# A two-layer trunk on one core: the weight sums begin after the rotated queries, and the bias rows are made in the plain stage

## The chip, the core and the metric

The kernel runs on one core of one Trainium2 chip. It uses the five engines of the core: PE (matrix products), DVE (vector), ACT (scalar functions and copies), POOL (a second vector engine) and SP, which here does nothing but issue transfers. ACT and POOL issue transfers too, each in its own queue and in the order of its other instructions. The metric is the time of one execution in device microseconds; less is better.

## The reference, cut to what matters

512 tokens of width 1024 go through two layers and a last norm. Layer 0 mixes tokens by two kinds of attention over all tokens, heads A (with rotated queries and keys) and heads B (through low-rank projections). Layer 1 uses a neighbourhood attention C whose scores get a bias from a small table, `od_rpb`, by the relative row and column of query and key. Each layer ends with an MLP with a squared ReLU.

```python
def sq_relu_mlp(h, w_up, w_down):
    u = jax.nn.relu(h @ w_up)
    return (u * u) @ w_down

h = x
for layer in range(2):
    hn = rmsnorm(h, norm_mix[layer])
    if layer % 2 == 0:
        h = h + hybrid_attention(hn, ...)            # heads A and B
    else:
        h = h + neighbourhood_attention(hn, od_w_qkv, od_rpb, od_w_out)
    h = h + sq_relu_mlp(rmsnorm(h, norm_ffn[layer]), ffn_w_up[layer], ffn_w_down[layer])
return rmsnorm(h, final_norm)
```

In the neighbourhood attention, `bias = rpb[:, kr - qr + ..., kc - qc + ...]` is added to the scaled scores of the keys in the window.

## The kernel before

Every fp32 product is made of three matmuls on PE: each operand is split into a rounded high part (`whi`, made by ACT) and the rest (`wlo`, made by DVE as operand minus high part).

The order of work is mostly that of the program; a scheduler puts each engine's instructions into a queue. The stages, with their times in the profile of before:

- **Heads A and B (from about 60 us on).** Per head and query tile: a pair of score matmuls (L1038), the exponential, transposes and value matmuls. Between them `fill` runs pieces of other products. `step(h, i)` is called once per head and tile. The queries of the second, third and fourth pair of heads are rotated on the way: SP swaps parts (L572), POOL multiplies (L576, L577), DVE adds, ACT rounds, DVE subtracts, and SP moves the halves into place by three transfers one after another (L649, L650, L651, in `sum_q`). The scores of those heads wait for the last of them; the tiles are named `a` and `sc`.
- **MLP, plain stage.** The first six row tiles of the up product and their part of the down product, as ordinary three-matmul products.
- **MLP, seven-product stage (about 328 to 482 us in layer 0, 900 to 1049 us in layer 1).** The rest of the up product goes by a scheme with seven block products instead of eight. It has 52 chunks in a layer. For each chunk (`seven_chunk`), SP loads a 128x2x256 piece of the weights (L300), POOL makes three sums of blocks (L302 to L304), ACT rounds (L308), DVE subtracts (L309), and PE runs 21 matmuls (L388 to L390).
- **MLP, sweeps (about 482 to 620 us in layer 0, from 1049 us on in layer 1).** The down product, in three kinds of sweep over pairs of row tiles kp (13 in layer 0, 11 in layer 1). It reads weights and sums of weight blocks from a tensor in device memory, `made`, splits them (L1310, L1311) and multiplies (L1413 to L1415).

**The sums ahead.** `SumsAhead` prepares `made` long before the sweeps. For each kp it issues two copies of 512 KB on ACT's queue (L809) and four accumulating transfers of 256 KB on POOL's (L803): two add a block of the weights (in the page `made<-in_ffn_w_down_dram`), and two add one block of `made` to another (`made<-made`), the second of which reads what the first wrote. It is a generator; `tick`, which every group of matmuls calls with its microseconds, advances it by one step when `every` microseconds have passed. These steps are the beats. For each kp the adds come one, two and three kp behind its copies, so that other steps lie between a transfer and the one that reads its result; where steps of one kind run out at the end of the list, the remaining adds follow one another directly. Both layers have such a list, `ahead0` with a beat of 4.7, set before the heads, and `ahead1` with 5.5.

**The bias rows.** `bias_rows` makes the rows of the bias for attention C: eight loads of the table by SP (L1264), two memsets and two copies on POOL (L1267 to L1271; L1270 copies a 128x128 part, L1271 a 128x248 part), and 48 stores to the device tensor `bx` on SP (L1276, L1280, L1282). In the kernel before, all of it is advanced by the sweeps of layer 0: one step for every fourth step of the sweeps of the second and third kind.

Working tiles come from a pool of 30 slots of 128x1024 elements (`Slot`) and from four raw buffers (`raw`); a chunk's load can go as soon as a slot is free and its place in SP's queue is reached.

Of the kernel before, what the change touches and what calls it, by code (L numbers as in the profile page):

```python
# [35 lines left out]
def encoder_kernel(ctx: ExitStack, tc: tile.TileContext, ins, out, dbg=None):  # L36
# [755 lines left out]
    class SumsAhead:  # L792
# [326 lines left out]
    def step(h, i):  # L1119
        n = count[0]  # L1120
        count[0] += 1
        if n == 35:
# [136 lines left out]
    def bias_rows():  # L1259
        held = tc.keep_in_program_order  # L1260
        R, Fi, Fe = Slot(F32), Slot(F32), Slot(F32)
        rpb = ins["od_rpb"][0]
        for qr in range(8):
            held(SP.dma_start(R.t[16 * qr : 16 * qr + 16, 0:248],  # L1264
                              rpb.rearrange("h a b -> h (a b)")[:, (7 - qr) * 31 : (7 - qr) * 31 + 248]))
            yield
        POOL.memset(Fi.t[:, 0:376], NEG)  # L1267
        POOL.memset(Fe.t[:, 256:512], NEG)
        rv = R.t[:, 0:248].rearrange("p (k d) -> p d k", d=31)
        POOL.tensor_copy(Fi.t[:, 0:376].rearrange("p (j k) -> p j k", k=8)[:, 15:31, :], rv[:, 7:23, :])  # L1270
        POOL.tensor_copy(Fe.t[:, 0:248].rearrange("p (j k) -> p j k", k=8), rv)  # L1271
        for _ in range(6):
            yield
        bxv = bx.rearrange("h t (c r) k -> t c r h k", r=8)
        for c in range(16):
            held(SP.dma_start(bxv[0, c].rearrange("r h k -> r h k"), Fi.t[:, (15 - c) * 8 : (15 - c) * 8 + 256]))  # L1276
# [3 lines left out]
            held(SP.dma_start(bxv[1, c][:, :, 128 * v : 128 * v + 128], Fe.t[:, off : off + 128]))  # L1280
            yield
            held(SP.dma_start(bxv[1, c][:, :, 128 - 128 * v : 256 - 128 * v], Fe.t[:, 256:384]))  # L1282
            yield
        for s_ in (R, Fi, Fe):
            s_.free()
        yield
# [192 lines left out]
    def mlp_swept(l, made, last=None):  # L1479
# [36 lines left out]
        for n, (kind, kp) in enumerate(sweeps[0].run(R)):  # L1516
# [3 lines left out]
            if kind and n % 4 == 0:  # L1520
# [266 lines left out]
    beat.update(every=5.5, work=ahead1.steps())  # L1787
# [169 lines left out]
```

## Time and profile before

| | |
|---|---|
| median of 3 executions | 1198.68 us (1196.86 to 1199.11) |
| the profiled execution | 1199.76 us |
| its span | 1197.9 us |
| PE busy | 1152.0 us, 96% |
| DVE busy | 905.0 us, 76% |
| ACT busy | 675.5 us, 56% |
| POOL busy | 527.5 us, 44% |

The span is the stretch from the first to the last instruction of one execution; 1.9 us of that execution lie outside it. A share over the span is a mean of stages: an engine with a small share can be the one that is waited for in one stage. A row of the timeline has the start in us, the duration, the engine, the line and the operation, and in brackets how long the engine was idle just before and what ended that. Rows at L803 on POOL, and rows of `SPq` and `ACTq`, are issues of transfers; their duration is that of the issue, not of the transfer.

### The profile page before, as it was taken

The numbers are of one execution on the slowest core, as the hardware profiler recorded it, in microseconds if no ns is written. First come the engines' busy times: TensorE is split into PE (matmuls) and PEld (weight loads), VectorE is DVE, ScalarE is ACT, GpSimd is POOL, SyncE is SP. The second block draws the span as 40 slices with busy tenths as digits, with TensorE's granted clock in tenths as the row PEclk, the third lists the DMA queues.
The fourth block names the chain that finished last, engine by engine and source line by source line (L and its number), as shares of the span: only waits on it lengthen the run. The fifth ranks groups of instructions, "written<-read, shape, count | busy, mean of one in ns | idle before, by whom it ended". The sixth has DMA issues, their size and how long they took to land.

```text
span 1197.9 us, 21331 instructions
## 1 busy us (share of the span) xinstructions
PE 1152.0 (96%) x7668; PEld 1040.3 (87%) x7668; DVE 905.0 (76%) x1627; ACT 675.5 (56%) x1157; POOL 527.5 (44%) x650
## 2 busy tenths in 40 slices
PE   9978999999999998998999999999999999999997
PEld 8657688888889998997998889988888999999995
DVE  5776899888967756994766566667889776699955
ACT  5456686665626655753653555554562665576625
POOL 3266454332699978032000332433169999800000
PEclk9998999999999998998999999999999999999999
DMA  7254464763876566826856867875667654685802
GB/s 250 62 146 114 131 159 102 180 141 109 242 188 157 152 131 131 292 84 205 256 155 169 228 184 185 196 170 154 195 158 212 161 138 121 154 254 177 265 10 70
DMA packets 131753, 197.33 MB, mean 165 GB/s; under 512 B 13011, under 2 KB 81536, under 8 KB 130880
## 3 DMA queue, kind: packets, MB, share of 16 engines
q1 hardware_dynamic: 113232, 138.18, 37.4%
q0 software_dynamic: 16128, 31.48, 16.5%
q10 hardware_dynamic: 2288, 26.32, 6.7%
q8 instruction: 60, 0.98, 0.4%
q14 instruction: 45, 0.37, 0.1%
HBM read 173.52 MB, written 56.62 MB: 192 GB/s over the span
## 4 chain that ended last, share of the span: by engine, by line
PE 64%; POOL 12%; DVE 10%; DMA 5%; issue 4%; ACT 3%; SPq 1%; ACTq 0%; POOLq 0%; DVEq 0%
PE mm L515 6%; PE mm L517 6%; PE mm L516 6%; POOL a L303 4%; POOL a L304 3%; PE s L1038 2%; POOL a L302 2%; PE t L1414 2%; PE t L1413 2%; PE t L1415 2%; PE o L1026 2%; PE t L1013 2%; POOL a L1270 1%; DMA raw<-in_ffn_w_down_dram 1%; PE s L516 1%
## 5 line engine op out<-in xcount | busy, mean ns | idle before, releaser
L309 DVE TENSOR_TENSOR wlo<-a,whi 128x896 fp32r<-128x896 f32 x98 | 121.5, 1241 | 72.9 <-ACT whi L308 66.8
L308 ACT ACTIVATE whi<-a 128x896 fp32r<-128x896 f32 x98 | 93.3, 952 | 129.7 <-POOL a L304 46.6
L515 PE MATMUL mm<-a,whi 128*128 128x512 f32 x395 | 160.0, 407 | 0.6 <-DVE sc L922 0.3
L517 PE MATMUL mm<-a,wlo 128*128 128x512 f32 x395 | 156.2, 396 | 0.4 <-DVE wlo L202 0.3
L516 PE MATMUL mm<-a,whi 128*128 128x512 f32 x395 | 156.2, 395 | 0.1
L202 DVE TENSOR_TENSOR wlo<-raw,whi 128x1024 fp32r<-128x1024 f32 (+4 forms) x87 | 100.7, 1162 | 32.1 <-ACT whi L212 32.0
L212 ACT ACTIVATE whi<-raw 128x1024 fp32r<-128x1024 f32 (+3 forms) x90 | 84.4, 942 | 66.1 <-PE s L516 13.6
L303 POOL TENSOR_TENSOR a<-a 128x256 f32<-128x256 f32 x98 | 95.2, 971 | 7.7
L517 PEld LDWEIGHTS mm<-a,wlo 128*128 128x128 f32 x395 | 74.4, 189 | 17.4 <-DVE wlo L202 1.3
L515 PEld LDWEIGHTS mm<-a,whi 128*128 128x128 f32 x395 | 74.4, 189 | 16.4 <-issue 1.1
L1046 POOL TENSOR_SCALAR p<-p,ti 128x512 f32<-128x512 f32 x64 | 47.8, 748 | 90.6 <-DVE ti L1045 72.1
L304 POOL TENSOR_TENSOR a<-a 128x128 f32<-128x128 f32 x98 | 84.2, 859 | 7.7
L302 POOL TENSOR_TENSOR a<-a 128x128 f32<-128x128 f32 x98 | 67.6, 690 | 44.6 <-DMA a<-in_ffn_w_up_dram 31.3
L516 PEld LDWEIGHTS mm<-a,whi 128*128 128x128 f32 x395 | 74.6, 189 | 13.5 <-DVE a L559 0.4
L388 PE MATMUL mm<-a,whi 128*128 128x256 f32 x280 | 79.7, 285 | 4.5 <-ACT whi L308 4.4
L1414 PE MATMUL t<-a,whi 128*128 128x256 f32 x288 | 81.0, 281 | 0.4 <-DVE a L1359 0.4
L390 PE MATMUL mm<-a,wlo 128*128 128x256 f32 x280 | 79.7, 284 | 1.6 <-DVE wlo L309 1.6
L1311 DVE TENSOR_TENSOR wlo<-a,whi 128x1024 fp32r<-128x1024 f32 x51 | 62.3, 1223 | 24.9 <-ACT whi L1310 24.8
L1413 PE MATMUL t<-a,whi 128*128 128x256 f32 x288 | 81.0, 281 | 0.0
L1415 PE MATMUL t<-a,wlo 128*128 128x256 f32 x288 | 80.7, 280 | 0.0
L389 PE MATMUL mm<-a,whi 128*128 128x256 f32 x280 | 79.4, 284 | 0.0
L1654 POOL TENSOR_SCALAR p<-p,ti 128x256 f32<-128x256 f32 x64 | 36.1, 575 | 96.7 <-DVE ti L1653 85.0
(395 smaller groups left out, 3927.8 us busy)
## 6 DMA issues: line engine op xcount, KB each, us to landing
a<-in_ffn_w_up_dram SPq DMA_DIRECT2D x98, 256.0 KB
made<-in_ffn_w_down_dram ACTq DMA_DIRECT2D x48, 512.0 KB
a<-made SPq DMA_DIRECT2D x74, 256.0 KB
made<-in_ffn_w_down_dram POOLq DMA_DIRECT2D x48, 256.0 KB, 5.3
made<-made POOLq DMA_DIRECT2D x48, 256.0 KB, 5.2
a<-in_ffn_w_down_dram SPq DMA_DIRECT2D x38, 256.0 KB
raw<-in_ffn_w_down_dram SPq DMA_DIRECT2D x34, 256.0 KB
raw<-in_ffn_w_down_dram SPq DMA_DIRECT2D x16, 512.0 KB
```

What stands on the lines that cost most here:

```text
L202: z = lambda: (eng or DVE).tensor_tensor(to, src, f32(high), op=ALU.subtract)
L302: POOL.tensor_tensor(r[:, 6], r[:, 0], r[:, 1], op=ALU.subtract)
L303: POOL.tensor_tensor(r[:, 4:6], r[:, 2:3].to_broadcast([P, 2, P]), r[:, 0:7:6], op=ALU.add)
L304: POOL.tensor_tensor(r[:, 7], r[:, 3], r[:, 5], op=ALU.subtract)
L308: ACT.activation(hi[:, 0:896], raw[:, 128:1024], AF.Copy)
L309: DVE.tensor_tensor(lo[:, 0:896], raw[:, 128:1024], f32(hi[:, 0:896]), op=ALU.subtract)
L515: PE.matmul(o, wh, xh, start=first, stop=False)
L516: PE.matmul(o, wh, xl, start=False, stop=False)
L517: PE.matmul(o, wl, xh, start=False, stop=last)
L1413: PE.matmul(o, wh, x[:, 0], start=first and m % 2 == 0, stop=False, skip_group_check=True)
L1414: PE.matmul(o, wh, x[:, 1], start=False, stop=False, skip_group_check=True)
L1415: PE.matmul(o, wl, x[:, 0], start=False, stop=last, skip_group_check=True)
```

## The change

There are two parts.

1. *The sums.* `ahead0` no longer begins before the heads: its beat is set in `step` at the count 20, which is the first query tile of head 5, right after the last rotated queries' transfers are in the program, and is 3.7 instead of 4.7. `ahead1`'s beat is 5.0 instead of 5.5. Behind the last kp's copies two empty beats are put ahead of each further kp's adds.
2. *The bias rows.* They take one slot, cut in three, instead of three slots. The POOL instructions are held in program order, one memset is 128 wide instead of 256, and the six empty steps between copies and stores are gone. Ten of the steps (the loads, the POOL work and the first store) are advanced in the plain stage's down product, and the other stores by every fifth step of the sweeps.

```diff
         def steps(self):
             for kp in range(self.n + 3):
+                if kp > self.n:
+                    yield
+                    yield
                 if kp < self.n:
                     for z in range(2):
                         tc.keep_in_program_order(ACT.dma_start(self.made[kp, z], self.w[kp, z]))
...
+        if n == 20:
+            beat.update(every=3.7, work=ahead0.steps())
         fill.run(1.5)
 
     ahead0, ahead1 = (SumsAhead(ins["ffn_w_down"][l], FIRST, RAW[l] // 2) for l in range(2))
-    beat.update(every=4.7, work=ahead0.steps())
...
     def bias_rows():
         held = tc.keep_in_program_order
-        R, Fi, Fe = Slot(F32), Slot(F32), Slot(F32)
+        slot = Slot(F32)
+        R, Fi, Fe = (slot.t[:, a:b] for a, b in ((0, 248), (248, 624), (624, 1008)))
         rpb = ins["od_rpb"][0]
         for qr in range(8):
-            held(SP.dma_start(R.t[16 * qr : 16 * qr + 16, 0:248],
+            held(SP.dma_start(R[16 * qr : 16 * qr + 16],
                               rpb.rearrange("h a b -> h (a b)")[:, (7 - qr) * 31 : (7 - qr) * 31 + 248]))
             yield
-        POOL.memset(Fi.t[:, 0:376], NEG)
-        POOL.memset(Fe.t[:, 256:512], NEG)
-        rv = R.t[:, 0:248].rearrange("p (k d) -> p d k", d=31)
-        POOL.tensor_copy(Fi.t[:, 0:376].rearrange("p (j k) -> p j k", k=8)[:, 15:31, :], rv[:, 7:23, :])
-        POOL.tensor_copy(Fe.t[:, 0:248].rearrange("p (j k) -> p j k", k=8), rv)
-        for _ in range(6):
-            yield
+        held(POOL.memset(Fi, NEG))
+        held(POOL.memset(Fe[:, 256:384], NEG))
+        rv = R.rearrange("p (k d) -> p d k", d=31)
+        held(POOL.tensor_copy(Fi.rearrange("p (j k) -> p j k", k=8)[:, 15:31, :], rv[:, 7:23, :]))
+        held(POOL.tensor_copy(Fe[:, 0:248].rearrange("p (j k) -> p j k", k=8), rv))
+        yield
...
         for c, gen in enumerate(gens):
             for i, _ in enumerate(gen):
                 later(c, i)
+                if i % 4 == 3 and c * 6 + i // 4 < 10:
+                    next(bias, None)
...
-            if kind and n % 4 == 0:
+            if kind and n % 5 == 0:
                 next(bias, None)
...
-    beat.update(every=5.5, work=ahead1.steps())
+    beat.update(every=5.0, work=ahead1.steps())
```

Lines shift: L1038 of before is L1041 of the change, L1267 to L1271 are L1272 to L1276, and the first store's L1276 is L1280. The rows below are read in the order in which the instructions stand in the queue of an engine. In them `a_3442` is the slot of the bias rows, `in_ffn_w_up_dram` the up product's weights, `made_621` and `made_622` are `made` of layer 0 and layer 1, and the other `a_` and `raw_` are chunks.

The first place is POOL's queue behind the sixth chunk of layer 0's seven-product stage. So it stands now; before, there was no instruction of the bias rows in this stage:

```order
L302 TENSOR_TENSOR a_3613<-a_3613 128x128
L303 TENSOR_TENSOR a_3613<-a_3613 128x256
L304 TENSOR_TENSOR a_3613<-a_3613 128x128
L1272 MEMSET a_3442 128x376
L1273 MEMSET a_3442 128x128
L1275 COPY a_3442<-a_3442 128x128
L1276 COPY a_3442<-a_3442 128x248
L803 DMA made_621<-in_ffn_w_down_dram 128x512
L302 TENSOR_TENSOR a_3690<-a_3690 128x128
L303 TENSOR_TENSOR a_3690<-a_3690 128x256
```

The two memsets and two copies have moved here from the sweeps, between two chunks' sums. In SP's queue the first store of `bx` that reads the result of these copies is followed by loads of chunks:

```order
L1280 DMA bx<-a_3442 8x16x256
L300 DMA raw_5040<-in_ffn_w_up_dram 128x2x256
L300 DMA a_3695<-in_ffn_w_up_dram 128x2x256
L300 DMA a_3726<-in_ffn_w_up_dram 128x2x256
L300 DMA raw_5169<-in_ffn_w_up_dram 128x2x256
L300 DMA a_3861<-in_ffn_w_up_dram 128x2x256
L300 DMA a_3825<-in_ffn_w_up_dram 128x2x256
```

Before, no store of `bx` stood among the loads of this stage.

The second place is POOL's queue near the end of that stage. Before:

```order
L803 DMA made_621<-in_ffn_w_down_dram 128x512
L302 TENSOR_TENSOR a_4786<-a_4786 128x128
L303 TENSOR_TENSOR a_4786<-a_4786 128x256
L304 TENSOR_TENSOR a_4786<-a_4786 128x128
L302 TENSOR_TENSOR a_4816<-a_4816 128x128
L303 TENSOR_TENSOR a_4816<-a_4816 128x256
L304 TENSOR_TENSOR a_4816<-a_4816 128x128
L803 DMA made_621<-made_621 128x512 x2
L302 TENSOR_TENSOR a_4884<-a_4884 128x128
L303 TENSOR_TENSOR a_4884<-a_4884 128x256
L304 TENSOR_TENSOR a_4884<-a_4884 128x128
L302 TENSOR_TENSOR a_4889<-a_4889 128x128
```

Now, at the place where the adds stand side by side:

```order
L803 DMA made_621<-made_621 128x512
L302 TENSOR_TENSOR a_4699<-a_4699 128x128
L303 TENSOR_TENSOR a_4699<-a_4699 128x256
L304 TENSOR_TENSOR a_4699<-a_4699 128x128
L803 DMA made_621<-made_621 128x512
L803 DMA made_621<-in_ffn_w_down_dram 128x512
L803 DMA made_621<-made_621 128x512
L302 TENSOR_TENSOR a_4768<-a_4768 128x128
L303 TENSOR_TENSOR a_4768<-a_4768 128x256
```

Before, two adds of `made` to `made` stood directly one behind the other, the second reading what the first writes; now one add stands after a single chunk's sums, followed further down by three adds in a row, of which the last reads what the one ahead of it writes.

The third place is POOL's queue in layer 1's seven-product stage, 13 chunks from its end. Before:

```order
L302 TENSOR_TENSOR a_11519<-a_11519 128x128
L303 TENSOR_TENSOR a_11519<-a_11519 128x256
L304 TENSOR_TENSOR a_11519<-a_11519 128x128
L803 DMA made_622<-made_622 128x512
L302 TENSOR_TENSOR a_11587<-a_11587 128x128
L303 TENSOR_TENSOR a_11587<-a_11587 128x256
L304 TENSOR_TENSOR a_11587<-a_11587 128x128
L302 TENSOR_TENSOR a_11592<-a_11592 128x128
```

Now:

```order
L302 TENSOR_TENSOR a_11389<-a_11389 128x128
L303 TENSOR_TENSOR a_11389<-a_11389 128x256
L304 TENSOR_TENSOR a_11389<-a_11389 128x128
L803 DMA made_622<-made_622 128x512 x2
L302 TENSOR_TENSOR a_11457<-a_11457 128x128
L303 TENSOR_TENSOR a_11457<-a_11457 128x256
L304 TENSOR_TENSOR a_11457<-a_11457 128x128
L302 TENSOR_TENSOR a_11462<-a_11462 128x128
```

The adds had a chunk or two of POOL's sums between them; now two of them stand side by side, and the second reads what the first writes. Fewer adds are left for the end of the stage.

More of the change, by code (lines that the diff above doesn't have):

```diff
@@ L1260, in bias_rows @@
         held = tc.keep_in_program_order
[L1261 removed]
+        slot = Slot(F32)
+        R, Fi, Fe = (slot.t[:, a:b] for a, b in ((0, 248), (248, 624), (624, 1008)))
         rpb = ins["od_rpb"][0]
         for qr in range(8):
[L1264 removed]
+            held(SP.dma_start(R[16 * qr : 16 * qr + 16],
                               rpb.rearrange("h a b -> h (a b)")[:, (7 - qr) * 31 : (7 - qr) * 31 + 248]))
             yield
[L1267 to L1273 removed]
+        held(POOL.memset(Fi, NEG))
[4 more added lines that the diff above has]
+        yield
         bxv = bx.rearrange("h t (c r) k -> t c r h k", r=8)
         for c in range(16):
[L1276 removed]
+            held(SP.dma_start(bxv[0, c].rearrange("r h k -> r h k"), Fi[:, (15 - c) * 8 : (15 - c) * 8 + 256]))
             yield
             v, off = (1, (7 - c) * 8) if c < 8 else (0, (23 - c) * 8)
[L1280 removed]
+            held(SP.dma_start(bxv[1, c][:, :, 128 * v : 128 * v + 128], Fe[:, off : off + 128]))
             yield
[L1282 removed]
+            held(SP.dma_start(bxv[1, c][:, :, 128 - 128 * v : 256 - 128 * v], Fe[:, 256:384]))
             yield
[L1284 to L1286 removed]
+        slot.free()
     def sweep_chunk(w, k0, kind, made):
```

## Prediction

> **What bounds the kernel now.** I read four views: the page's first part for the bound, the table of stretches for where the bound has holes, the list of PE's waits for what opens them, and the timeline around each hole. The first says that TensorE is the bound.
>
> ```profile
> span 1197.9 us, 21331 instructions
> PE 1152.0 (96%) x7668; PEld 1040.3 (87%) x7668; DVE 905.0 (76%) x1627; ACT 675.5 (56%) x1157; POOL 527.5 (44%) x650
> ```
>
> PE misses 1197.9 - 1152.0 = 45.9 us, and the change leaves its work alone: before and after it issues the same matmuls, in another order only among the heads of attention A. So the change can win at most part of 45.9 us, plus what half clock stretches, and can lose without limit. The stretches (columns: length, then busy time with instruction count of PE, PEld, DVE, ACT, POOL, then granted clock, DMA share, GB/s) show the holes:
>
> ```profile
> 60.00:90.00 30.00, 21.30 (x101) 15.35 (x99) 22.90 (x53) 16.14 (x33) 18.09 (x17) 1.00 0.55 146
> 90.00:120.00 30.00, 24.73 (x130) 21.17 (x131) 19.52 (x46) 18.20 (x41) 19.37 (x23) 0.85 0.46 115
> 390.00:420.00 30.00, 30.00 (x256) 30.00 (x255) 23.25 (x29) 18.70 (x23) 28.43 (x35) 1.00 0.61 159
> 420.00:450.00 30.00, 27.43 (x228) 26.81 (x226) 15.90 (x18) 15.05 (x17) 23.96 (x32) 1.00 0.58 124
> 450.00:480.00 30.00, 27.12 (x204) 26.82 (x205) 20.49 (x25) 17.36 (x21) 25.10 (x33) 0.89 0.64 136
> 540.00:570.00 30.00, 24.10 (x184) 23.40 (x183) 14.88 (x22) 12.01 (x18) 5.41 (x2) 0.89 0.67 214
> 990.00:1020.00 30.00, 30.00 (x258) 30.00 (x256) 19.43 (x24) 16.95 (x19) 28.27 (x37) 1.00 0.53 132
> 1020.00:1050.00 30.00, 28.09 (x231) 27.27 (x230) 20.51 (x24) 17.89 (x21) 23.03 (x30) 1.00 0.70 158
> 1110.00:1140.00 30.00, 30.00 (x256) 30.00 (x255) 26.68 (x40) 19.07 (x30) 0.00 (x0) 1.00 0.79 261
> ```
>
> Holes: heads A (60-120), the end of layer 0's seven-product stage (420-480), layer 0's sweeps (540-570), and a small one in layer 1's seven-product stage (1020-1050). POOL reads 28.43 and 28.27 of 30 in the two seven-product stages: it has no room there, whatever its 44% over the span says. Three waits open the large holes:
>
> ```profile
> PE s L1038 <- DMA a<-sc: 6.5, 2, 4.3
> PE mm L1413 <- ACT whi L1310: 4.7, 1, 4.7
> PE mm L388 <- ACT whi L308: 4.4, 1, 4.4
> ```
>
> Each of them also halves the granted clock for some time after (same columns):
>
> ```profile
> 90.00:97.00 7.00, 4.87 (x19) 4.40 (x20) 3.06 (x7) 1.67 (x4) 1.68 (x3) 0.52 0.32 78
> 117.00:121.00 4.00, 4.00 (x17) 3.27 (x16) 3.34 (x8) 2.52 (x6) 3.75 (x5) 0.58 1.02 258
> 452.00:459.00 7.00, 6.12 (x27) 5.83 (x28) 4.33 (x5) 2.61 (x4) 6.61 (x9) 0.51 0.42 81
> 551.00:558.00 7.00, 4.31 (x18) 4.02 (x19) 1.58 (x2) 2.07 (x3) 0.00 (x0) 0.51 0.92 314
> ```
>
> At clock 0.51, PE's 6.12 us hold about 6.12 x 0.49 = 3.0 us of work lost; the others 4.87 x 0.48 = 2.3, 4.00 x 0.42 = 1.7 and 4.31 x 0.49 = 2.1. A hole thus costs its idle time and some 2 to 3 us behind it.
>
> **Heads A: the sums leave.** Layer 0's sums started with the heads; now none is issued before head 5's first score. What PE waits for there is the rotation of the next queries, a relay of small transfers on SP's queue (L649 to L651), and L651 moves what the last copies need:
>
> ```profile
> 83.16 0.50 SPq L649 DMA_DIRECT2D a<-a  x1
> 87.67 0.46 SPq L651 DMA_DIRECT2D a<-sc  x1
> 92.13 1.65 PE L1038 MATMUL s<-a,a 128*128 128x512 f32 x3 [4.28 <-DMA a<-sc]
> 109.23 0.50 SPq L649 DMA_DIRECT2D a<-a  x1
> 113.11 0.46 SPq L651 DMA_DIRECT2D a<-sc  x1
> 116.70 0.73 PE L1038 MATMUL s<-a,a 128*128 128x512 f32 x2 [2.22 <-DMA a<-sc]
> ```
>
> The first relay takes 92.13 - 83.16 = 8.97 us, the second 116.70 - 109.23 = 7.47. Part of the difference is traffic: the first runs beside copies and sums, which now are gone. POOL, which makes the products that the rotation sums (L577), is not held by an add either, as it was here:
>
> ```profile
> 69.93 0.90 POOL L803 DMA_DIRECT2D made<-in_ffn_w_down_dram  x1 [0.73 <-DMA made<-in_ffn_w_down_dram]
> 70.55 1.58 POOL L577 TENSOR_TENSOR sc<-sc,a 128x512 f32<-128x512 f32 x1
> ```
>  The fill moves too: between the last scores of unrotated queries and the first that needs rotated ones, PE now has 11 matmuls of fill, 18 transposes and 16 value matmuls where it had 6, 12 and 9. The two waits, 6.5 us in sum, and the dips behind them, 2.3 and 1.7, are what can go: 10.5. Bounds: -10.5, and nothing, since the relay itself remains and 7.47 us of it is there with few sums beside it. I take **-6**, a little over half: the first wait loses 8.97 - 7.47 = 1.5 by the relay and more by the fill, and with it its dip; the second is left half of its 2.2 and 1.7.
>
> [...]
>
> **Layer 0's seven-product stage: POOL gets more.** A chunk here costs POOL three sums (L302 to L304), then ACT rounds, DVE subtracts, and PE multiplies. POOL's rows around the hole, with PE's:
>
> ```profile
> 443.32 0.81 POOL L803 DMA_DIRECT2D made<-made  x1
> 448.84 0.81 POOL L803 DMA_DIRECT2D made<-made  x1 [4.71 <-DMA made<-made]
> ...
> 453.89 0.81 POOL L803 DMA_DIRECT2D made<-made  x1
> 454.45 0.72 POOL L302 TENSOR_TENSOR a<-a 128x128 f32<-128x128 f32 x1
> ```
>
> ```profile
> 452.49 0.58 PE L388 MATMUL mm<-a,whi 128*128 128x256 f32 x1 [4.41 <-ACT whi L308]
> ```
>
> An add followed by the add that reads its result stands in POOL's order with nothing between; POOL waits 4.71 us for the first one's landing, and PE then waits 4.41. An add that does not wait costs POOL 454.45 - 453.89 = 0.56 us of its order. The change:
> - *The bias rows' memsets and copies* now stand behind the sixth chunk. Their durations are on these rows:
>
> ```profile
> 527.97 16.84 POOL L1270 COPY a<-a 128x128 f32<-128x128 f32 x1 [9.69 <-DMA a<-in_od_rpb_dram]
> 544.76 0.65 POOL L1271 COPY a<-a 128x248 f32<-128x248 f32 x1
> 528.00:544.80 16.80, 16.80 (x145) 16.80 (x144) 16.54 (x35) 10.55 (x21) 16.80 (x2) 1.00 0.05 17
> 340.00:350.00 10.00, 10.00 (x55) 8.54 (x54) 5.16 (x6) 1.91 (x2) 9.37 (x15) 1.00 0.93 240
> ```
>
>   The first copy took 16.84 us while DVE was busy 16.54 of 16.80; the second, with nearly twice the elements, 0.65 once DVE had stopped. Where they go now, DVE is busy 5.16 of 10. Bounds: 2 x 0.65 with DVE away, 16.84 + 0.65 with DVE full. 5.16 is a half-empty DVE, so I take the low end and double it, 2.7 us with the two memsets (an estimate, not rowed for the memsets).
> - *Adds*: 24 instead of 21 stand between the third and the last chunk: 3 x 0.56 = +1.7.
> - *Pairs*: the adjacent pair that waited 4.71 is gone, and another takes its place three chunks earlier (an add and the one that reads it, adjacent); one pair with only one chunk between is new. That chunk takes POOL some 2.6 us of a landing of about 4.71 + 0.81 = 5.5, so +2.5. These waits may come out between 0 and 4.71.
> - *SP's queue*: the first store of the rows waits for POOL's copy with seven weight loads behind it; with raw buffers loaded ahead I cost it at nothing. If the copy is as slow as 16.84, all of that cover is gone and it comes on top.
>
> Together POOL's end of the stage moves by 2.7 + 1.7 + 2.5 = 6.9. PE ran full until 420 (30.00 of 30), so POOL's lead of the early chunks hides little; I take **+6.5**, between +1 (POOL early enough, pairs landed) and +15 (slow copy).
>
> [...]
>
> **Layer 0's sweeps: the copy leaves.** The rows of that hole:
>
> ```profile
> 544.84 0.72 SPq L1276 DMA_DIRECT2D bx<-a  x1
> 547.02 1.82 SPq L1304 DMA_DIRECT2D a<-made  x4
> 553.23 0.58 PE L1413 MATMUL mm<-a,whi 128*128 128x256 f32 x1 [4.69 <-ACT whi L1310]
> ```
>
> The slow copy ended at 544.81, the store that needs it went at 544.84, and only then SP reached the sweep's loads at 547.02. PE misses 30 - 24.10 = 5.9 us in 540-570, about 1.1 behind it, and 2.1 at half clock: 9.1. With the copies done a stage earlier, SP's stores wait on nothing of POOL's. Layer 1's sweeps have no bias rows, and there PE is at 30.00 of 30 (1110-1140, DMA share 0.79). The stores' own issue time (0.72 us above) is spread more thinly (every fifth step). Bounds: -9.1 and -6 (a few loads late). I take **-8.6**.
>
> **Layer 1's seven-product stage.** With a beat of 5.0 for 5.5 the adds come earlier. Before, none waited in the stage, as this shows:
>
> ```profile
> 1042.64 1.65 POOL L803 DMA_DIRECT2D made<-made  x2
> 1049.44 0.81 POOL L803 DMA_DIRECT2D made<-made  x1 [5.15 <-DMA made<-made]
> ```
>
> The 5.15 us wait stands behind the last chunk and holds nobody. Now a pair stands adjacent inside the stage, 13 chunks from its end: up to 5.15 us of POOL, less the one add fewer (22 for 23, -0.56): +4.6. PE idles 1.9 there before (1020-1050), so POOL's lead is small but not zero until about 1020; I take **+4**, between -1 (landed in time, fewer adds late) and +7 (with a clock dip as above).
>
> **The plain stages and the tail** I cost at nothing. The sums' traffic of layer 0 is compressed by 4.7 / 3.7 = 1.27 in time after the heads, beside full PE (cover: loads issued ahead); uncovered, one late load would be a wait as in the sweeps, up to 4.7. The empty beats act after the last kp has been copied.
>
> **Sum**, against the profiled execution (1199.76 us, 1.1 above the median of 1198.68): -6 + 6.5 - 8.6 + 4 = -4.1, so 1195.7, rounded to 1195.5.
>
> **Rivals.**
> - *POOL's lead covers.* Both new waits land in time and the copies are short, so layer 0's stage costs +1 and layer 1's 0: -6 - 8.6 + 2 = -12.6, 1187. For it: before, PE did not idle until after 420, so a lead exists. Against: 28.43 of 30 busy.
> - *Slower: the copy meets DVE.* In its new place the first copy (L1275 of the change) runs long as L1270 did. Price: 16.84 for some 1.3, 15.5 more on POOL; if a lead of two chunks (5.5) covers a part, +10, so -4.1 + 10 = +6, 1206. It decides from a copy of some 5.4 us on, where the sum of -4.1 is eaten. For it: the old row. Against: DVE 5.16 of 10.
> - *The relay is the wait, not the traffic.* The heads' waits stay as they are (the change doesn't do there what it moves the sums for): term 0, sum +1.9, 1202. For it: 7.47 us in the relay with few sums beside it. Against: more fill ahead of the first such score.
>
> **How the numbers follow.** Forecast 0.45 (own range 1190 to 1201), POOL's lead 0.22, relay 0.18, copy 0.15. About what this kernel's measurement can tell is 0.2%, 2.4 us. Faster: 0.7 of the forecast and all of the lead, 0.54. Within: a quarter of the forecast and half of the relay, 0.20. Slower: the rest, 0.26. The range reaches to the two outer rivals, 1186 to 1206.
>
> **What would show it.** Right: no L803 on POOL before the sixth head, and the row at L1038 that waits for a<-sc under 3 us with no half clock behind it; the first copy (L1275) under 2 us, in the seven-product stage; no store of bx in the sweeps that waits for POOL and 540-570 above 29; in both seven-product stages a wait of PE at L388 of 2 to 6 us behind an L803 of 3 to 5. Wrong: a copy of over 5 us, PE full in the seven-product stages, or the relay's waits unchanged.

## The result, and the profile after

The changed kernel takes 1193.05 us (median of 5, 1192.06 to 1194.29) against 1198.68 us before (5 runs, 1196.86 to 1200.67): a ratio of 0.9953 with a 95% interval of 0.9939 to 0.9968. The forecast was 1195.5 us, with a range of 1186 to 1206 and faster as the likelier sign.

The page's first part of the kernel after, and then its two largest waits of PE (us in total, times, longest):

```profile
span 1192.5 us, 21335 instructions
PE 1152.1 (97%) x7668; PEld 1039.8 (87%) x7668; DVE 900.7 (76%) x1627; ACT 674.1 (57%) x1157; POOL 509.1 (43%) x650
```

```profile
PE s L388 <- ACT whi L308: 6.6, 1, 6.6
PE mm L390 <- DVE wlo L309: 4.5, 9, 1.1
```

PE has as much to do as before (1152.1 us), so all of the 5.4 us are holes closed or opened. The two waits for the rotated queries (6.5 us) and the wait in the sweeps (4.7 us) are gone from the list; the one at L388 in the seven-product stage is still there and has grown from 4.4 to 6.6. The stretches (columns as before: length, busy time of PE, PEld, DVE, ACT, POOL, granted clock, DMA share, GB/s):

```profile
60.00:90.00 30.00, 25.99 (x125) 19.45 (x123) 25.80 (x61) 19.49 (x39) 18.65 (x18) 0.94 0.21 55
90.00:120.00 30.00, 28.56 (x164) 22.53 (x164) 25.06 (x64) 25.38 (x58) 23.73 (x27) 1.00 0.34 89
150.00:180.00 30.00, 26.13 (x149) 22.34 (x148) 24.37 (x59) 21.90 (x49) 14.62 (x19) 0.94 0.71 176
420.00:450.00 30.00, 20.91 (x150) 19.39 (x149) 12.31 (x15) 11.28 (x14) 21.59 (x30) 0.90 0.63 114
540.00:570.00 30.00, 30.00 (x256) 30.00 (x255) 25.48 (x40) 18.62 (x30) 0.00 (x0) 1.00 0.73 232
990.00:1020.00 30.00, 28.58 (x237) 27.95 (x236) 18.69 (x21) 16.39 (x20) 25.32 (x33) 1.00 0.51 116
```

Heads A and the sweeps are fuller, 420-450 emptier. Fixed stretches mislead once the kernels have shifted against each other, so I also cut each profiled execution at the same pieces of work: the first matmul of each seven-product stage (L388), the first and the last matmul of each down product's sweeps. The lengths of the pieces, in us (layer 0's seven-product stage so begins at 347.5 us in the kernel before, later than in the list of stages, since the other engines work on its chunks ahead of PE):

| piece | before | after | difference | forecast |
|---|---|---|---|---|
| start to layer 0's seven-product stage | 347.5 | 340.4 | -7.0 | -6 |
| layer 0's seven-product stage | 138.2 | 148.0 | +9.8 | +6.5 |
| layer 0's sweeps | 139.2 | 128.9 | -10.3 | -8.6 |
| to layer 1's seven-product stage | 296.2 | 298.1 | +1.9 | 0 |
| layer 1's seven-product stage | 131.7 | 132.2 | +0.5 | +4 |
| layer 1's sweeps and the tail | 145.1 | 144.9 | -0.2 | 0 |
| sum, of the span | | | -5.4 | -4.1 |

The signs of the four terms came out as forecast; one of them, +0.5, is too small to tell from the spread between profiles (below). The stretch of layer 0's seven-product stage, cut so, before and after:

```profile
347.47:485.69 138.22, 132.76 (x1094) 131.85 (x1092) 97.12 (x115) 81.16 (x100) 117.62 (x148) 0.98 0.63 152
```

```profile
340.44:488.42 147.98, 135.41 (x1094) 131.93 (x1092) 99.88 (x119) 81.24 (x101) 122.84 (x154) 0.98 0.67 163
```

PE stands idle there for 5.5 us before and 12.6 us after, and its 1094 matmuls take 2.65 us longer. Half clock does not explain these 2.65 us: the granted clock is 0.98 in both rows, and the stretch at half clock is not longer than the one before the change (452 to 459 us, 6.12 us of matmuls):

```profile
444.00:450.83 6.83, 4.46 (x19) 4.17 (x20) 3.44 (x4) 3.07 (x4) 6.44 (x10) 0.50 0.35 76
```

What lengthens the other matmuls is not shown. The timeline of the kernel after shows the hole, POOL first and then PE:

```profile
427.47 0.81 POOL L803 DMA_DIRECT2D made<-made  x1
432.03 0.81 POOL L803 DMA_DIRECT2D made<-made  x1 [1.16 <-DMA made<-made]
434.62 0.80 POOL L803 DMA_DIRECT2D made<-made  x1
435.16 1.09 POOL L803 DMA_DIRECT2D made<-in_ffn_w_down_dram  x1
442.32 0.81 POOL L803 DMA_DIRECT2D made<-made  x1 [6.06 <-DMA made<-in_ffn_w_down_dram]
```

```profile
445.98 0.58 PE L388 MATMUL s<-a,whi 128*128 128x256 f32 x1 [6.63 <-ACT whi L308]
```

The last of three adds in a row waits 6.06 us for the one just ahead of it, and PE 6.63 for the chunk behind. Two adds with one chunk between wait 1.16.

### The profile page after: what moved, and what is told of

Its sections match the earlier page's. It is cut to its first block, busy times and chain, and to the rows that moved or that the text cites. A ratio compares the mean times of both kernels' runs of the same rounds, so it can differ in the third digit from the quotient of the medians.

```text
span 1192.5 us, 21335 instructions
## 1 busy us (share of the span) xinstructions
PE 1152.1 (97%) x7668; PEld 1039.8 (87%) x7668; DVE 900.7 (76%) x1627; ACT 674.1 (57%) x1157; POOL 509.1 (43%) x650
## 4 chain that ended last, share of the span: by engine, by line
PE 69%; POOL 12%; DVE 7%; DMA 4%; issue 4%; ACT 3%; ACTq 0%; POOLq 0%; SPq 0%; DVEq 0%
PE mm L515 6%; PE mm L517 6%; PE mm L516 6%; POOL a L303 5%; POOL a L304 3%; POOL a L302 3%; PE t L1416 3%; PE t L1415 3%; PE t L1417 3%; PE s L1041 3%; PE o L1029 2%; PE t L1016 2%; PE mm L1417 2%; DMA a<-in_ffn_w_up_dram 2%; PE mm L1415 2%
## 5 line engine op out<-in xcount | busy, mean ns | idle before, releaser
L308 ACT ACTIVATE whi<-a 128x896 fp32r<-128x896 f32 x95 | 89.6, 949 | 121.0 <-POOL a L304 59.2
L303 POOL TENSOR_TENSOR a<-a 128x256 f32<-128x256 f32 x95 | 89.3, 943 | 7.3
L302 POOL TENSOR_TENSOR a<-a 128x128 f32<-128x128 f32 x95 | 72.3, 764 | 40.8 <-DMA a<-in_ffn_w_up_dram 40.3
L1566 POOL DMA_DIRECT2D a<-a x16 | 8.7, 547 | 179.3 <-PE mm L516 164.4
L1313 DVE TENSOR_TENSOR wlo<-a,whi 128x1024 fp32r<-128x1024 f32 x56 | 68.3, 1222 | 21.3 <-ACT whi L1312 20.9
L388 PE MATMUL mm<-a,whi 128*128 128x256 f32 x280 | 78.7, 281 | 0.2 <-ACT whi L308 0.2
```

The lines of the kernel that those rows point to most:

```text
L302: POOL.tensor_tensor(r[:, 6], r[:, 0], r[:, 1], op=ALU.subtract)
L303: POOL.tensor_tensor(r[:, 4:6], r[:, 2:3].to_broadcast([P, 2, P]), r[:, 0:7:6], op=ALU.add)
L308: ACT.activation(hi[:, 0:896], raw[:, 128:1024], AF.Copy)
```

## The experiments

The theory to be tested: four places, each with its own cause, whose effects add; and in the seven-product stages the cost is the wait of an add for the one issued just before it. The main rivals: POOL's whole work paces those stages, so that the wait only shows where the lack falls; and what one place gains, the next gives back.

Each experiment's time stands beside runs of the kernel before on the same chip (medians 1197.8 to 1198.3), and the ratio is to these.

### Each part alone

Only the sums' part (the bias rows as before):

```diff
-    beat.update(every=4.7, work=ahead0.steps())
+        if n == 20:
+            beat.update(every=3.7, work=ahead0.steps())
... (and the empty beats, and 5.0 for 5.5)
```

> Only the change's part on the sums (start at head 5's first score, beats 3.7 and 5.0, empty beats); the bias rows as before, made and stored in the sweeps. By the theory (four places, each with its own cause, that add): heads A gain 7 us as in the change, the sweeps keep their whole hole (first wait of about 4.7 us at L1413 behind a POOL copy of about 17 us), and layer 0's seven-product stage has an adjacent dependent pair of adds at chunk 39, so it stays near its 138 us or rises by up to 5: 1192 to 1197, near 1194. Rival (the heads' gain is only idle time that the next stages give back, so the sum is set by the stages' POOL): within 2 us of the kernel before.

Measured: 1194.92 us (10 runs), ratio 0.9975 (0.9955 to 0.9995). The sweeps keep their hole, as the rows of its timeline show, POOL's and then PE's:

```profile
528.98 17.87 POOL L1274 COPY a<-a 128x128 f32<-128x128 f32 x1 [8.65 <-DMA a<-in_od_rpb_dram]
```

```profile
554.57 0.39 PE L1417 MATMUL mm<-a,whi 128*128 128x256 f32 x1 [4.00 <-ACT whi L1314]
```

Its sweeps take 137.8 us, and its seven-product stage 140.7, with a wait of POOL of 5.42 us at an adjacent pair and one of PE of 5.95 us behind it. Its profiled execution, the slowest of the ten, gains almost nothing up to the stage (346.9 us), mostly because of one wait of 4.54 us for a transfer in heads B that the other kernels with the sums begun at head 5 show at 0 to 1.8 us. So the gain of the heads cannot be read from this profile.

Only the bias rows' part (the sums as before):

```diff
+        slot = Slot(F32)
+        R, Fi, Fe = (slot.t[:, a:b] for a, b in ((0, 248), (248, 624), (624, 1008)))
... (and the steps in the plain stage, stores on every fifth step)
```

> Only the change's part on the bias rows; the sums as before (start ahead of the heads, beats 4.7 and 5.5, no empty beats). By the theory the sweeps of layer 0 gain the 10 us that they gain in the change, heads A keep their two waits on the rotated queries (about 4.3 and 2.2 us), and the seven-product stage pays 2.3 us of POOL for the memsets and copies, with its adjacent pair of adds now at chunk 32 instead of 43, where PE still has a lead: stage +0 to +4, total 1188 to 1193, near 1190.5. Rival (what the sweeps gain, the seven-product stage loses, since POOL is full there): 1196 to 1199. If the two parts add, the gains of this run and of the one with the sums alone come to more than the 5.6 us of both together by what the two share, the pair of adds in the stage.

Measured: 1191.87 us, ratio 0.9949 (0.9927 to 0.9971). In the profiled execution, the slowest of the ten (1197.57 us), the sweeps take 129.1 us (139.2 before) and the stage 142.2. The memsets and copies, of which the first copy took 16.84 us in the sweeps, here among the chunks of the seven-product stage:

```profile
340.99 0.41 POOL L1268 MEMSET a<- 128x376 f32 x1
341.34 0.20 POOL L1269 MEMSET a<- 128x128 f32 x1
341.49 0.42 POOL L1271 COPY a<-a 128x128 f32<-128x128 f32 x1
341.85 0.65 POOL L1272 COPY a<-a 128x248 f32<-128x248 f32 x1
```

Its stage has its own adjacent pair, at chunk 32 instead of 43. POOL waits there about as long as in the kernel before (4.71 us), PE much less (4.41 before):

```profile
422.75 0.81 POOL L803 DMA_DIRECT2D made<-made  x1 [4.34 <-DMA made<-made]
```

```profile
426.44 0.39 PE L388 MATMUL s<-a,whi 128*128 128x256 f32 x1 [1.39 <-ACT whi L308]
```

So what a pair costs PE hangs on its place. PE's longest wait in this stage, 3.04 us at 369.51, is of another kind. It stands near the stage's start, where the kernel before has no idle time. SP had stood for 12.5 us at the first store of the bias rows, so a chunk's load went late, and POOL waited for it:

```profile
343.12 0.38 SPq L300 DMA_DIRECT2D raw<-in_ffn_w_up_dram  x1
```

```profile
351.00 0.46 POOL L302 TENSOR_TENSOR raw<-raw 128x128 f32<-128x128 f32 x1 [4.34 <-DMA raw<-in_ffn_w_up_dram]
```

From there POOL works without a pause, and PE's wait at 369.51 ends with the chunk whose sums POOL finished at 368.5.

The two parts alone gain 3.4 and 6.4 us, 9.8 together; with both, 5.6. They share layer 0's seven-product stage, and there they do not add: it is 2.5 and 4.0 us longer than before with one part each (in the slowest executions of both) and 9.8 with both.

### The adjacent pair: the same change with another beat

A scheduler places the adds between POOL's sums, and the beat's number moves them all. With 3.6 and with 3.8 for layer 0's sums, no add stands next to the one whose result it reads, in either layer's stage; the adds are as many.

```diff
-            beat.update(every=3.7, work=ahead0.steps())
+            beat.update(every=3.6, work=ahead0.steps())
```

> The change with a beat of 3.6 instead of 3.7 for layer 0's sums: as many adds, but no add stands next to the one whose result it reads in either seven-product stage (in the change one pair does in each: waits of POOL of 6.1 and 3.3 us). Theory (the pair is what costs layer 0's stage its 10 us: 6.6 us of PE's wait at L388 and some 3 us of half clock): no wait of PE over 1.5 us at L388, the stage near 139 to 141 us instead of 148, total 1184 to 1187. Rival (POOL's whole work paces the stage, 31 adds and the bias rows beside the chunks; the pair only says where the lack shows): many small waits in its place, stage 145 to 148, total 1190 to 1193.

> The change with a beat of 3.8 instead of 3.7: again no adjacent dependent pair in either stage, but one more of the adds falls into the last chunks. Theory (the pair): as with 3.6, 1184 to 1187, and the two agree within 2 us although their beats lie on both sides of 3.7. Rival (POOL's whole work, or the beat itself, since slower beats leave more adds late): 1190 to 1193, or a time that moves with the beat.

Measured: 1178.66 us with 3.6, ratio 0.9834 (0.9812 to 0.9856), and 1178.71 us with 3.8, ratio 0.9839 (0.9809 to 0.9868). Both are 14.4 us better than 3.7, which lies between them, and they agree to 0.1 us: a slower or faster pace is not what gains here. In the profile with 3.6, the stage:

```profile
339.69:477.20 137.51, 132.12 (x1094) 129.77 (x1092) 96.86 (x118) 80.05 (x100) 117.72 (x151) 1.00 0.66 162
```

It is 10.5 us shorter than in the change: 7.2 us less idle time of PE and 3.3 us less matmul time, at a full clock. The rows of the change trace most of that to the pair: PE's wait of 6.63 us and, by the prediction's reckoning, 4.46 x 0.50 = 2.2 us of work lost at half clock, 8.9 together. Layer 1's stage is 129.1 us instead of 132.2. Around the place of the old wait POOL now has

```profile
430.11 0.81 POOL L803 DMA_DIRECT2D made<-in_ffn_w_down_dram  x1
430.66 1.10 POOL L803 DMA_DIRECT2D made<-made  x1
431.21 1.39 POOL L302 TENSOR_TENSOR a<-a 128x128 f32<-128x128 f32 x1
```

Two adds stand side by side again, and there is no wait: the second does not read what the first writes. It is the dependence that costs here, 6.06 us in the change, not that they stand together.

The gain is larger than either theory had it (1184 to 1187, 1190 to 1193). Of the 15.2 us between the two spans, 10.5 lie in layer 0's stage and 3.1 in layer 1's; the expectation had left out the second.

### The pair in layer 1 alone

With 3.5 the pair stands in layer 1's stage only.

> The change with a beat of 3.5 for layer 0's sums: no adjacent dependent pair in layer 0's seven-product stage, but layer 1's stage has its pair 13 chunks from the end, as in the change. So it prices layer 1's pair alone, against 3.6 and 3.8 (1178.7), which have neither. Theory from the stages' lengths (layer 1's stage 132.2 us with the pair, 129.1 without): 1181 to 1183. Rival (PE's lead in layer 1 hides the pair and the 3 us are something else): 1177 to 1180.

Measured: 1186.93 us, ratio 0.9906 (0.9887 to 0.9925). POOL's row at the pair:

```profile
989.59 0.80 POOL L803 DMA_DIRECT2D made<-made  x1
993.72 0.81 POOL L803 DMA_DIRECT2D made<-made  x1 [3.33 <-DMA made<-made]
```

Layer 1's stage takes 132.6 us, 3.5 more than with 3.6 and 3.8 (129.1). But the other kernels with a beat of 5.0 and no pair there spread up to 130.8 us, and the three with the pair from 132.2 to 132.7; so the pair's price in layer 1 is some 1.4 to 3.8 us, for waits of POOL of 3.3 to 3.8. The total is higher than either forecast, because layer 0's stage takes 143.1 us, 5.6 more than with 3.6, without any waiting add: POOL waits there 1.31 us twice at chunks' sums near the start, and PE once 2.26 us, with a lower clock behind it (0.83 from 360 to 380 us). So pairs are not all that a beat decides.

### Pairs one chunk apart: without the empty beats

```diff
-                if kp > self.n:
-                    yield
-                    yield
```

> The change without the empty beats: pairs of dependent adds remain at two places of layer 0's stage, each with one chunk's sums between them; none adjacent, in neither layer. Theory (the wait is what the landing, some 5 to 6 us, is longer than the work between the two adds): each costs POOL 1 to 3 us, of which PE sees part: stage 139 to 143 us, total 1179 to 1185. Rival (the empty beats are what keeps dependent adds apart, so without them it is worse): over 1193.

Measured: 1190.04 us (6 runs, 1182.05 to 1194.05), ratio 0.9924 (0.9892 to 0.9955). Its two pairs, with one chunk between, wait 1.25 and 2.39 us, as the theory had it:

```profile
431.68 0.81 POOL L803 DMA_DIRECT2D made<-made  x1 [1.25 <-DMA made<-made]
...
456.80 0.81 POOL L803 DMA_DIRECT2D made<-made  x1 [2.39 <-DMA made<-made]
```

Its stage takes 144.1 us, longer than the 139 to 143 expected, and the total lies between the two forecasts. No single wait of PE in the stage is over 1.2 us, and yet the stage is 6.6 us longer than with 3.6; how much of that is the two pairs is not shown. The empty beats do not by themselves help: with the beat at 3.7 the kernel without them is no slower than with them (0.9924 against 0.9953).

### The kernel before, and the bias part, without the pair

With 4.8 for 4.7 the kernel before has no adjacent pair in layer 0's stage.

```diff
-    beat.update(every=4.7, work=ahead0.steps())
+    beat.update(every=4.8, work=ahead0.steps())
```

> The kernel before with one number changed: layer 0's beat 4.8 instead of 4.7. Then no add stands next to the one whose result it reads in layer 0's seven-product stage, and layer 1 is as it was. Bias rows and the sums' start ahead of the heads stay. Theory (the adjacent pair alone makes the hole of layer 0's seven-product stage): that stage falls from 138 us by the 4.4 us wait and some of the 3 us of half clock behind it, heads and sweeps keep their holes: 1190 to 1193. Rival (POOL's whole work paces it): stage within 1.5 us of before, 1197 to 1199.

Measured: 1197.81 us (10 runs), ratio 0.9992 (0.9977 to 1.0008). The stage falls by the 4 us that the theory had, from 138.2 to 134.1:

```profile
351.43:485.50 134.07, 130.87 (x1093) 129.64 (x1092) 96.48 (x114) 79.59 (x98) 119.54 (x151) 1.00 0.65 152
```

but it begins at 351.4 instead of 347.5, and the total does not move: the forecast of 1190 to 1193 missed. Where the heads lose these 4 us is spread over 120 to 180 us; it isn't one wait, and why a beat of 4.8 costs them is left open. The rival that what one place gains another gives back fits this run, only that the loss comes ahead of the gain.

The bias part with 4.8:

> The change's part on the bias rows alone, with layer 0's beat 4.8 instead of 4.7, so that no adjacent dependent pair is left in the stage; the sums begin ahead of the heads as before. Against the change with a beat of 3.6 or 3.8 (1178.7) it lacks only the late start of the sums and the empty beats. Theory (four places that add): those heads cost about 7 us, so 1184 to 1187. Rival (the late start is worth nothing by itself, only the pairs and the bias rows count): 1178 to 1181.

Measured: 1187.23 us, ratio 0.9904 (0.9881 to 0.9928). Up to the stage it takes 351.1 us, the stage 133.6, the sweeps 129.6. It is some 8.5 us slower than the change with 3.6, a little more than the theory had (1184 to 1187), and what it mainly lacks is the late start (339.7 us up to the stage, 11.4 less), against a shorter stage. It also keeps layer 1's beat of 5.5, which its expectation leaves out; layer 1's stage takes 130.3 us, 1.2 more than with 3.6.

### The sums begun at the count 9

```diff
-        if n == 20:
+        if n == 9:
```

> The change with the sums begun at the count 9 (right after the first relay of rotated queries) instead of 20, beat 3.7 as in the change; no adjacent dependent pair in either stage. The second and third relay run beside the sums' copies again. If the sums' traffic is what slows a relay, the second or third relay takes some 7.5 to 9 us and PE waits 2 to 4 us at the scores behind it: 1181 to 1184. If a relay is slow only where POOL or SP are held ahead of it, or only where PE lacks fill, no score waits for the relay: 1178 to 1180.

Measured: 1190.36 us, ratio 0.9932 (0.9906 to 0.9958), slower than both forecasts. Up to the stage it takes 348.5 us, as much as before the change, though the first relay runs without the sums. The rows of the third relay, SP's in this kernel, and then in the change:

```profile
127.75 0.50 SPq L649 DMA_DIRECT2D a<-a  x1
...
132.26 0.46 SPq L651 DMA_DIRECT2D a<-sc  x1
```

```profile
121.76 0.51 SPq L649 DMA_DIRECT2D a<-a  x1
...
123.99 0.46 SPq L651 DMA_DIRECT2D a<-sc  x1
```

From the first to the last issue 4.5 us pass beside the sums and 2.2 without, and PE then waits 2.07 us at the scores (134.82). So a relay is slower here beside the sums, as the first theory had it. It is not all of the 8 us that the kernel loses up to the stage: at the 65th score matmul it is already 9.6 us behind the change (168.8 against 159.2), of which this wait explains 2. The rest stays open.

### What POOL's work ahead of the stage is worth

The bias steps on every second step of the plain stage, so that the copies stand ahead of the third chunk, with a beat of 3.6:

```diff
-                if i % 4 == 3 and c * 6 + i // 4 < 10:
+                if i % 2 == 1 and c * 12 + i // 2 < 10:
```

> The change with a beat of 3.6 and the bias rows' steps advanced every second step of the plain stage's down product instead of every fourth, so that POOL's memsets and copies stand before the third chunk, where POOL waits for PE anyway, instead of behind the sixth. The adds stand exactly as with 3.6 alone (1178.7). Theory (POOL paces layer 0's stage, and its 2.3 us of memsets and copies are paid in full): stage 2 us shorter, 1176 to 1177.5. Rival (the 2.3 us are hidden by PE's lead): within 1 us of 1178.7.

Measured: 1178.58 us, ratio 0.9835 (0.9818 to 0.9851): no difference from 1178.66, and the stage takes 138.1 us for 137.5. Moving the 2.3 us of memsets and copies ahead gains nothing. POOL's time from the third chunk to the last is 3.7 us shorter, and PE's idle time in the late part, from 418 to 438 us, is the same (2.58 and 2.65 us). Near the stage's start something is left all the same: in its first 21 us PE is idle for 1.93 us here and 1.06 with 3.6. All eleven kernels that make the bias rows ahead of the sweeps have such idle time, 0.5 to 3.5 us, and the three that make them in the sweeps have none. So the bias rows do cost this stage something. With the bias rows alone it came by SP's wait at the first store; but here that wait is only 1.3 us and PE idles all the same, so it isn't the only way.

Then 3.2, which has four adds fewer among chunks 3 to 51:

> The change with a beat of 3.2: no adjacent dependent pair in either stage, and 19 instead of 23 adds among chunks 3 to 51 of layer 0's stage, since the list ends earlier; its traffic in heads B and in the plain stage is denser by 3.6 / 3.2. Theory (POOL paces the stage at 0.57 us an add): stage 2.3 us shorter than with 3.6, if the heads do not grow: 1175.5 to 1177.5. Rival (denser traffic costs the heads what the stage gains, as with the start at 9): 1179 to 1184.

Measured: 1179.82 us, ratio 0.9847 (0.9828 to 0.9866). The late part is fuller and the early one emptier:

```profile
343.71:480.37 136.66, 131.97 (x1094) 130.74 (x1092) 101.30 (x120) 80.45 (x100) 113.93 (x148) 0.99 0.61 156
363.23:382.76 19.53, 17.45 (x134) 17.25 (x135) 13.98 (x15) 13.36 (x17) 18.43 (x24) 0.91 0.62 157
421.80:441.32 19.52, 18.93 (x157) 18.52 (x157) 11.12 (x13) 10.85 (x12) 18.42 (x24) 1.00 0.53 116
```

and it reaches the stage 4 us later than with 3.6 (343.7 against 339.7): the rival's case. Both edits together:

> A beat of 3.2 together with the bias rows' steps on every second step of the plain stage. Alone, each moved the time by about 1 us or less: 3.2 freed the late part of layer 0's stage (PE's idle time from 421 to 461 us 0.9 us instead of 3.5) and lost at its start (3.8 us of idle time, with the loads late there), and the early copies freed POOL ahead of the stage. Theory (the lead at the start of the stage is what 3.2 lacks): the start is mended, stage about 134, total 1176 to 1178. Rival (the lead is capped by the slots and by the loads, so early POOL work is not banked): 1179 to 1180.5.

Measured: 1181.78 us (5 runs, 1178.52 to 1188.64), ratio 0.9854 (0.9835 to 0.9873), slower than both forecasts. In the profiled execution, the slowest of the five, the start was not mended: PE waits 7.41 us at L388 at 367 us. That early work of POOL is not banked fits this; for the other four executions there is no profile.

## Why the prediction was right, point by point

**The total.** The forecast was 3.2 us of gain, and 5.6 were measured. That it came so near is in part luck: the term of layer 0's seven-product stage was 3.3 us too small and that of layer 1's 3.5 too large, and the two errors cancel.

**What bounds.** PE's work did not change (1152.0 and 1152.1 us), and all the difference is in holes: as said.

**Heads A, -6.** Measured -7.0. The kernels that start the sums at head 5 reach the stage at 339.3 to 343.7 us (eight of nine profiles; the ninth is the execution with the late transfer), those that start them ahead of the heads at 347.5 to 351.4 (four). The first relay, from the issue at L649 to that at L651, took 2.2 us where it had taken 4.5, and no score waited for it:

```profile
83.50 0.50 SPq L649 DMA_DIRECT2D a<-a  x1
85.72 0.46 SPq L651 DMA_DIRECT2D a<-sc  x1
```

The prediction's rival "the relay is the wait, not the traffic" is refuted in that its waits did not stay. What is not shown is how much of the 7 us is the relay and how much the order of the work beside it; the start at 9 suggests that the relay is the smaller part. In 60 to 90 us a dip appears behind another wait, 2.38 us (74.69), with a clock of 0.94, and of 0.61 from 74.6 to 78; before, a wait of 2.89 us at the same place (74.27) left the clock at 1.00. Another dip follows a wait of 2.16 us at 156 (0.94 in 150 to 180, and 0.50 from 158 to 160). So "under 3 us", which the prediction took as a sign of no half clock, is no safe sign. The prediction's own row showed it: the wait of 2.22 us at 116.70 was followed by a clock of 0.58 from 117 to 121 us, so it was not only the waits of 4.28 to 4.7 us that did it. The length of one wait did not decide it here: behind 2.16, 2.22 and 2.38 us the clock fell, and behind 2.89 it did not. What decides is not shown. The row of before and that of the change:

```profile
74.27 0.74 PE L1038 MATMUL s<-a,a 128*128 128x512 f32 x2 [2.89 <-DVE ti L1042]
```

```profile
74.69 0.73 PE L1041 MATMUL s<-a,a 128*128 128x512 f32 x2 [2.38 <-DVE ti L1045]
```

**Layer 0's sweeps, -8.6.** Measured -10.3, and all kernels agree: 128.6 to 129.6 us in the eleven that make the copies earlier, 137.8 to 139.4 in the three that make them in the sweeps. No store waits for POOL there, and 540-570 is at 30.00 of 30. The store that does wait for POOL now stands in the seven-product stage, where the prediction costed it at nothing. SP's rows there, and its wait in the list of SP's waits:

```profile
319.29 1.53 SPq L300 DMA_DIRECT2D a<-in_ffn_w_up_dram  x2
332.99 0.72 SPq L1280 DMA_DIRECT2D bx<-a  x1
334.14 0.38 SPq L300 DMA_DIRECT2D raw<-in_ffn_w_up_dram  x1
```

```profile
SPq L1280 <- POOL a L1275: 12.1, 1, 12.1
```

SP stands for 12.1 us with chunk loads behind it, POOL then waits 0.44 and 1.40 us for loads, and PE is idle for 1.97 us of the stage's first seventh, where it had no idle time before. That is a small price, but it isn't nothing; with the bias rows alone it was 3.04 us.

**Layer 0's seven-product stage, +6.5.** Measured +9.8, and here the working was wrong although the sum was near. The prediction let the new adjacent pair replace the old one at no cost. The copies in the change:

```profile
332.05 0.41 POOL L1272 MEMSET a<- 128x376 f32 x1
332.40 0.20 POOL L1273 MEMSET a<- 128x128 f32 x1
332.55 0.42 POOL L1275 COPY a<-a 128x128 f32<-128x128 f32 x1
332.91 1.53 POOL L1276 COPY a<-a 128x248 f32<-128x248 f32 x1
334.38 0.81 POOL L803 DMA_DIRECT2D made<-in_ffn_w_down_dram  x1
```

The sizes: copies and memsets 2.33 us (332.05 to 334.38), the pair with a chunk between 1.16, the adjacent pair 6.06 instead of 4.71.

The step that failed is that replacement. Without an adjacent pair the stage takes 134.1 us with the sums and the bias rows as before (4.8) and 137.5 us with both as in the change (3.6). So the rest of the change adds 3.4 us here, half of the 6.5, and the pairs 6.4: the old one cost 4.1 by this comparison (138.2 against 134.1), the new one 10.5 (148.0 against 137.5). Each of these numbers is from one profile, and kernels without an adjacent pair reach 143.1 (3.5) and 144.1 us (without the empty beats), so they are rough.

The prediction's other step, that PE loses about as much as POOL's work grows, is neither borne out nor refuted. Moving the copies out of the stage gained nothing; but with pairs one chunk apart, and waits of POOL of only 1.25 and 2.39 us, the stage is 6.6 us longer than with 3.6. What the rows do show is that a single long wait of POOL late in the stage goes to PE nearly whole (4.71 and 4.41 us before, 5.42 and 5.95 with the sums alone, 6.06 and 6.63 in the change), with half clock behind it (0.51 from 452 to 459 us before, 0.50 from 444 to 450.83 in the change), and one at chunk 32 does not (4.34 and 1.39 with the bias rows alone).

The second copy, which took 0.65 us in the sweeps, took 1.53 here, beside one subtraction of DVE:

```profile
332.58 1.34 DVE L309 TENSOR_TENSOR wlo<-a,whi 128x896 fp32r<-128x896 f32 x1
```

The copy stands from 332.91 to 334.44 and ends 0.52 us after that subtraction; with the bias rows alone DVE was idle at this place (340 to 343 us), and the copy took 0.65. In the sweeps, where DVE was busy for 16.54 of 16.80 us, the first copy had taken 16.84 us, and 17.87 in the sweeps of the kernel with the sums' part alone. That DVE's work is what lengthens a copy is my inference from these rows; no run shows it by itself, and in the change the first copy took 0.42 us (332.55 to 332.97) beside the same subtraction.

**Layer 1's stage, +4.** Measured +0.5. The pair waited 3.27 us where 5.15 was taken, and no wait of PE of 2 to 6 us came of it, as the prediction's sign had it: PE's longest wait at the chunks is 0.56 us, and it is idle for 1.66 us in all, against 1.91 before. Without a pair the stage takes 129.0 to 130.8 us with a beat of 5.0, and 130.0 to 132.1 in the four kernels with 5.5. So the faster beat seems to gain a little there, and the pair takes it back; the term hid two effects, each about as large as the spread between profiles.

**Costed at nothing.** The piece from the sweeps to layer 1's stage is 1.9 us longer than before. Over all the profiles here it varies from 294.8 to 298.5 us and follows no edit; I leave it.

**The rivals.** "POOL's lead covers" (1187; its terms of +1 and 0 are added as 2, so by its own terms 1186) did not come true for this program, but it named what decides, that the dependent adds land in time; where another beat lets them, the time is 8 us below its 1187. "The copy meets DVE" did not occur at the price given: beside DVE's subtraction the first copy took 0.42 us and the second 1.53, 0.9 more than in the sweeps.

## What to carry to other kernels

Where a scheduler places transfers that depend on one another among an engine's work, look in the engine's order for pairs of which the second reads the first's result, and move the number that spaces them before judging it: here 3.6 and 3.8 are 1.2% better than 3.7 between them. A table of lengths cut at the same pieces of work tells a change's terms apart where fixed stretches of time do not. Price a wait on a helper engine by its place: here 4.34 us of POOL at chunk 32 cost PE a wait of 1.39 us, and 6.06 us at chunk 40 one of 6.63.

## What the runs showed that was not expected

- The change with a beat of 3.6 or 3.8 is faster than the change itself: 1178.66 us with 3.6, a ratio of 0.9834 (0.9812 to 0.9856) to the kernel before, where the change as it stands has 0.9953.
- With a wait of 6.06 us on POOL late in layer 0's stage the stage is 10.5 us longer than without; waits of 3.3 to 3.8 us in layer 1's go with 1.4 to 3.8 us.
- Bias rows made beside layer 0's seven-product stage leave PE idle for 0.5 to 3.5 us in its first 21 us, in all eleven kernels; the prediction had that at nothing.
- From the issue of an add to the start of the next one, which waits for it, 7.2 us passed in layer 0 (435.16 to 442.32) and 4.1 us in layer 1 (997.09 to 1001.17). The prediction's 5.5 lay between.
- One number of the beat moves up to 4 us in the heads (347.5 to 351.4 us with 4.8 for 4.7), where the amount of work is the same; no single wait explains it, and this stays open.
